# One layer of a gated encoder with three branches on one Trainium2 core: memory keys and values kept unsplit in DRAM, branch input loaded at other products, nine small buffers

## The chip, the cores and the metric

The kernel runs on one core of a Trainium2 chip. The metric is the device time of one launch, in microseconds. It is compared by the median of several runs. The engines carry short names in every table: PE is TensorE (matmuls and transposes; PEld is its loading of weights), DVE is VectorE, ACT is ScalarE, POOL is GpSimd and SP is SyncE, which here only issues DMAs. [...]

## The reference, cut to what matters

One layer is applied to two groups with the same weights: a prompt of 1024 tokens and a sample of 512, each 1024 wide, each with its own 256 memory tokens.

```python
def cross_attention(xq, mem_n, w_mem_kv):
    kv = mem_n @ w_mem_kv                                   # 256 x 1024
    mk = kv[..., :X_WIDTH].reshape(B, M, N_X_HEADS, X_HEAD_DIM)
    mv = kv[..., X_WIDTH:].reshape(B, M, N_X_HEADS, X_HEAD_DIM)
    q = xq.reshape(B, L, N_X_HEADS, X_HEAD_DIM)
    s = jnp.einsum('blhd,bmhd->bhlm', q, mk) * (X_HEAD_DIM ** -0.5)
    p = jax.nn.softmax(s, axis=-1)
    return jnp.einsum('bhlm,bmhd->blhd', p, mv).reshape(B, L, X_WIDTH)

def encoder_layer(x, mem, ...):
    z = rms_norm(x, ln_pre) @ w_in        # cut into inputs and gates of the branches, and merge logits
    ...
    cross_out = cross_attention(xq, rms_norm(mem, ln_mem), w_mem_kv)
    branches = (pool_out * silu(pool_gate), attn_out * silu(attn_gate), cross_out * silu(x_gate))
    gates = sigmoid(merge_logits.reshape(B, L, 3, 1024) + b_merge)
    merged = sum(gates[:, :, n] * (branches[n] @ w_branch[n]) for n in range(3))
    return x + rms_norm(merged @ w_out, ln_post)
```

## The kernel before

All data is float32. Most products are made of three matmuls: both operands are split into a rounded high part and the rest, and `mm3` adds high times high, high times low and low times high (L127). The function `split` makes the two parts: ScalarE writes the high part as a copy (L166), VectorE subtracts it from the original (L163). The parts are kept in tiles of 128 x 2048 (`M`, 14 buffers) for activations, and in `whi` and `wlo` for weights, which `weights` loads into `raw` and splits.

Tiles come from pools that rotate: `U` (128 x 1024, seven buffers), `M`, `HU` (128 x 512, eight buffers, tag hu), `RAW`, and small ones for statistics (`S(n)`, one set of eight for each number of columns). A new tile waits until all readers of the buffer's former content are done. In PSUM `A` has three tiles of 128 x 1024 and `B` two of 128 x 512.

The program is written once in the order of the stages, and a scheduler puts each engine's instructions into a fixed order from it, with priorities (`tc.high_priority`) that pull some of them forward. Each engine works through its own list strictly in order, SP through its list of DMAs too.

The stages, in order of time:

1. `mem_phase` computes keys and values of the memory for both groups, some 10 to 75 us, woven with the steps of `long_h`, which normalises the prompt's input and makes the seven operands of a fast scheme of block products (`put` splits them; L267 and L280 are its differences and sums). Keys: four products of 128 x 512 in PSUM; `evacuate(c)` multiplies each by the norm (L720) into a tile of HU, splits it into two more, and stores high and low parts side by side into DRAM (`mkd`, one tensor for each group, 128 x 2048). Values: four products; ScalarE scales each into its high part (L759), VectorE makes the low part (L760), both are stored (`mvd`).
2. Projections of the prompt and of the sample (`products`, `plain`), 80 to about 700 us. The sums of L336 to L339 and the additions of L441 belong to them.
3. `stream`: a list of units, attention first, then cross attention of the two prompt blocks, attention of the sample, cross attention of the sample. Each unit goes through five steps at fixed distances (load ahead, scores, hand, turn, values), and between the steps matmuls of the remaining projections fill TensorE. In attention the weights of a row block are normalised by POOL and copied by a DMA from one U tile into another (`hand`, L819) before TensorE transposes them. `cross(b, ...)` has four units, one for each head c. `ahead(c)` loads the queries of a head into HU and splits them (L950, L951); at c = 0 it also loads the keys, high and low in one load of 1 MB into an M tile, at c = 2 the values likewise. So they are loaded three times each: for prompt block 0, prompt block 1 and the sample. `scores(c)` multiplies (12 matmuls of 256 columns), ScalarE takes exponentials (L972), POOL normalises (L976), `turn` transposes and splits, `values(c)` multiplies and gates (L998) and the result goes to DRAM as the third branch's output.
4. `branches` and `merge`: for each of three blocks of 512 tokens and each branch in the order 0, 2, 1, eight products (d = 0 to 7) of the branch's output with its weights; L1063 multiplies each by its merge gate, POOL adds (L1065). `chunk(n, c)` loads a quarter (256 KB) of branch n's output into an M tile; the four are split at d = 0 of that branch (`split_pair`). The next branch's chunks are loaded at d = 4 to 7 of the branch before. `gate(i)` loads a merge gate into HU two products ahead. The first block begins as filling of the stream's end.

All loads, and most stores, are issued by SP, in one list (L140 for every load).

## Time and profile before

| | us |
|---|---|
| median of 3 runs | 1477.14 (1474.91 to 1478.22) |
| the profiled execution | 1473.83 |
| its span, first to last instruction | 1472.0 |
| TensorE busy | 1435.9 (98%) |
| VectorE busy | 964.4 (66%) |
| ScalarE busy | 710.6 (48%) |
| GpSimd busy | 277.1 (19%) |

The mean granted clock is 0.993. The core moves 244.94 MB by DMA, at a mean of 166 GB/s. A busy time is the sum of an engine's instructions, so a TensorE that is busy at half its clock counts as busy; the time between the last instruction of the profile and the end of the execution, 1.83 us, lies outside the span. In a timeline row the first number is the start in us from the start of the span, the second the length of the piece, x2 that two instructions of one kind follow each other, and a bracket the idle time ahead with what released it.

### The profile page before, as it was taken

The numbers are of one execution on the slowest core, as the hardware profiler recorded it, in microseconds if no ns is written. First come the engines' busy times: TensorE is split into PE (matmuls) and PEld (weight loads), VectorE is DVE, ScalarE is ACT, GpSimd is POOL, SyncE is SP. The second block draws the span as 40 slices with busy tenths as digits, with TensorE's granted clock in tenths as the row PEclk, the third lists the DMA queues.
The fourth block names the chain that finished last, engine by engine and source line by source line (L and its number), as shares of the span: only waits on it lengthen the run. The fifth ranks groups of instructions, "written<-read, shape, count | busy, mean of one in ns | idle before, by whom it ended". The sixth has DMA issues, their size and how long they took to land. (4 is left out here: it accounts for less than half of the span.)

```text
span 1472.0 us, 19616 instructions
## 1 busy us (share of the span) xinstructions
PE 1435.9 (98%) x7264; PEld 1201.5 (82%) x7264; DVE 964.4 (66%) x1215; ACT 710.6 (48%) x1085; POOL 277.1 (19%) x286
## 2 busy tenths in 40 slices
PE   7989999999999999999999999999999999999998
PEld 5868888888888888788888888888888788888887
DVE  6986586666647674565777676666676564664664
ACT  6454444544434545443666666666666233233232
POOL 1001020110000000210223322233333150240231
PEclk9989999999999999999999999999999999999999
DMA  7523234341422443244655665585356844954852
GB/s 282 158 65 108 86 115 129 108 136 59 130 88 72 152 144 123 85 161 160 244 188 196 215 229 194 189 285 188 128 201 209 295 133 143 316 213 150 318 177 84
DMA packets 97391, 244.94 MB, mean 166 GB/s; under 512 B 10896, under 2 KB 20240, under 8 KB 96528
## 3 DMA queue, kind: packets, MB, share of 16 engines
q1 hardware_dynamic: 88080, 210.14, 42.9%
q10 hardware_dynamic: 9216, 33.56, 5.9%
q8 instruction: 57, 0.93, 0.3%
q14 instruction: 38, 0.31, 0.1%
HBM read 155.57 MB, written 54.53 MB: 143 GB/s over the span
## 5 line engine op out<-in xcount | busy, mean ns | idle before, releaser
L127 PE MATMUL B<-med,whi 128*128 128x512 f32 x1576 | 493.0, 393 | 7.7 <-DVE med L1063 2.8
L127 PE MATMUL A<-med,whi 128*128 128x512 f32 x1200 | 375.8, 394 | 1.9 <-DVE med L163 1.7
L127 PEld LDWEIGHTS B<-med,whi 128*128 128x128 f32 x1576 | 292.0, 188 | 68.2 <-DVE med L1063 3.2
L127 PE MATMUL B<-med,wlo 128*128 128x512 f32 x788 | 308.7, 392 | 0.5 <-DVE wlo L163 0.5
L163 DVE TENSOR_TENSOR wlo<-raw,whi 128x1024 fp32r<-128x1024 f32 (+1 forms) x169 | 205.8, 1218 | 143.5 <-ACT whi L166 140.3
L166 ACT ACTIVATE whi<-raw 128x1024 fp32r<-128x1024 f32 (+1 forms) x169 | 167.2, 990 | 272.1 <-PE A L127 125.5
L127 PEld LDWEIGHTS A<-med,whi 128*128 128x128 f32 x1200 | 224.2, 189 | 48.8 <-DVE med L163 2.2
L127 PE MATMUL A<-med,wlo 128*128 128x512 f32 x600 | 235.5, 392 | 1.8 <-DVE wlo L163 1.8
L127 PEld LDWEIGHTS B<-med,wlo 128*128 128x128 f32 x788 | 148.3, 188 | 32.8 <-DVE wlo L163 1.3
L163 DVE TENSOR_TENSOR med<-A,med 128x1024 fp32r<-128x1024 f32 (+1 forms) x93 | 112.9, 1215 | 34.1 <-ACT med L166 32.6
L127 PEld LDWEIGHTS A<-med,wlo 128*128 128x128 f32 x600 | 113.4, 189 | 26.2 <-DVE wlo L163 2.1
L188 POOL TENSOR_SCALAR s<-s 128x16 f32<-128x16 f32 (+3 forms) x17 | 7.5, 444 | 667.6 <-DVE s L581 332.5
L166 ACT ACTIVATE med<-A 128x1024 fp32r<-128x1024 f32 x92 | 94.2, 1025 | 76.4 <-PE A L131 76.0
L812 POOL TENSOR_SCALAR u<-u,s 128x1024 f32<-128x1024 f32 x64 | 72.2, 1128 | 211.7 <-DVE s L811 173.6
L1065 POOL TENSOR_TENSOR med<-med,hu 128x512 f32<-128x512 f32 x48 | 77.4, 1627 | 131.6 <-DVE hu L1063 127.6
L808 DVE TENSOR_REDUCE s<-A 128x1 f32<-128x1024 f32 x64 | 77.9, 1217 | 36.5 <-PE A L127 14.4
L127 PE MATMUL A<-whi,med 128*128 128x512 f32 (+1 forms) x352 | 98.2, 360 | 0.0
L810 ACT ACTIVATE u<-A,s 128x1024 f32<-128x1024 f32 x64 | 71.4, 1115 | 40.8 <-issue 23.3
L127 PE MATMUL A<-kt,med 128*128 128x512 f32 x320 | 87.9, 396 | 0.0
L166 ACT ACTIVATE whi<-sum 128x1024 fp32r<-128x1024 f32 x50 | 53.1, 1061 | 68.3 <-PE B L127 36.0
L166 ACT ACTIVATE med<-med 128x1024 fp32r<-128x1024 f32 (+1 forms) x44 | 44.2, 1018 | 76.4 <-POOL med L1065 37.1
L163 DVE TENSOR_TENSOR med<-med,med 128x1024 fp32r<-128x1024 f32 (+1 forms) x50 | 56.4, 1141 | 35.1 <-ACT med L166 31.3
(200 smaller groups left out, 1915.4 us busy)
## 6 DMA issues: line engine op xcount, KB each, us to landing
raw<-wt SPq DMA_DIRECT2D x168, 512.0 KB, 3.7
u<-u ACTq DMA_DIRECT2D x64, 512.0 KB, 3.2
merge<-hu SPq DMA_DIRECT2D x72, 256.0 KB, 2.1
hu<-merge SPq DMA_DIRECT2D x72, 256.0 KB, 4.7
med<-br SPq DMA_DIRECT2D x36, 256.0 KB, 4.9
q<-hu SPq DMA_DIRECT2D x24, 256.0 KB, 2.4
br<-hu SPq DMA_DIRECT2D x24, 256.0 KB, 2.7
med<-q SPq DMA_DIRECT2D x12, 512.0 KB, 4.9
```

The lines of the kernel that those rows point to most:

```text
L127: pe.matmul(out, l, r, **k)
L163: v.tensor_tensor(out, x, hi.bitcast(F32), op=ALU.subtract)
L166: act.activation(hi, x, AF.Copy)
L188: pool.tensor_scalar(ss, ss, EPS, 1.0, op0=ALU.add, op1=ALU.mult)
L808: v.reduce_max(mx[:], a[:], axis=AX.X, negate=True)
L810: act.activation(p, a[:], AF.Exp, bias=mx[:], accum_out=sm[:])
L812: pool.tensor_scalar(p, p, rc[:], 1.0, op0=ALU.mult, op1=ALU.mult)
L1065: pool.tensor_tensor(at, at, sg[:], op=ALU.add)
```

## The change

Memory keys and values: `evacuate` and the loop at the end of `mem_phase` store the unsplit product. `mkd` and `mvd` have half the size. `cross` loads them into a U tile at c = 0 (keys) and c = 2 (values) and splits them into an M tile at c = 1 and c = 3. A dictionary that both prompt blocks share keeps the split tiles, so block 1 neither loads nor splits; the sample has its own. Branch input: chunks are loaded at d = 2 to 5 instead of 4 to 7. Buffers: HU has nine instead of eight, and the small tiles of 1, 2 and 4 columns share one set of ten.

```diff
     def S(n):
-        return st.tile([P, n], F32, tag=f"s{n}", bufs=3 if n == 16 else 8, name=nm("s"))
+        w, bufs = (16, 3) if n == 16 else (4, 10)
+        return st.tile([P, w], F32, tag=f"s{w}", bufs=bufs, name=nm("s"))[:, :n]
...
         def evacuate(c):
-            t, hi, lo = HU(), HU(F32R), HU(F32R)
+            t = HU()
             with tc.high_priority(EVAC):
                 v.tensor_tensor(t[:], b[c], sp[:], op=ALU.mult)
-                split(hi[:], lo[:], t[:])
             for g in range(2):
-                for s, x in enumerate((hi, lo)):
-                    o = s * D + c * NMEM
-                    nc.sync.dma_start(mkd[g][:, o:o + NMEM], x[:, g * NMEM:(g + 1) * NMEM].bitcast(F32))
+                nc.sync.dma_start(mkd[g][:, c * NMEM:(c + 1) * NMEM], t[:, g * NMEM:(g + 1) * NMEM])
...
         for t in range(TT):
-            hi, lo = HU(F32R), HU(F32R)
+            x = HU()
             with tc.high_priority(EVAC):
-                act.activation(hi[:], b[t], AF.Copy, scale=r[:, t:t + 1])
-                v.scalar_tensor_tensor(lo[:], b[t], r[:, t:t + 1], hi[:].bitcast(F32), op0=ALU.mult, op1=ALU.subtract)
-            for s, x in enumerate((hi, lo)):
-                o = s * D + t % 2 * BLK
-                nc.sync.dma_start(mvd[t // 2][:, o:o + BLK], x[:].bitcast(F32))
+                act.activation(x[:], b[t], AF.Copy, scale=r[:, t:t + 1])
+            nc.sync.dma_start(mvd[t // 2][:, t % 2 * BLK:(t % 2 + 1) * BLK], x[:])
...
-            if c in (0, 2):
-                k, src = ("mk", mkd) if c == 0 else ("mv", mvd)
-                t = M()
-                load(t[:].bitcast(F32), src[:])
-                state[k] = [t[:, i * D:(i + 1) * D] for i in range(2)]
+            k, src = ("mk", mkd) if c < 2 else ("mv", mvd)
+            if c % 2 == 0 and k not in mem:
+                mem[k] = U()
+                load(mem[k], src[:])
+            elif c % 2 and not isinstance(mem[k], list):
+                t, x = M(), mem[k]
+                mem[k] = [t[:, i * D:(i + 1) * D] for i in range(2)]
+                split(*mem[k], x)
...
-                if d >= 4 and n != order[-1]:
-                    chunk(order[order.index(n) + 1], d - 4)
+                if 2 <= d < 6 and n != order[-1]:
+                    chunk(order[order.index(n) + 1], d - 2)
...
-    units += [u for b in range(2) for u in cross(b, sc, mkd[1], mvd[1])]
-    units += pairs_of(scs, kts, vts) + cross(0, scs, mkd[0], mvd[0])
+    mem = {}
+    units += [u for b in range(2) for u in cross(b, sc, mkd[1], mvd[1], mem)]
+    units += pairs_of(scs, kts, vts) + cross(0, scs, mkd[0], mvd[0], {})
...
-NU, NM, NHU, NRAW, NW = 7, 14, 8, 3, 2
+NU, NM, NHU, NRAW, NW = 7, 14, 9, 3, 2
```

Line numbers move by one or two: L163 becomes L164, L166 becomes L167, L267 becomes L268, L441 becomes L442, L1063 becomes L1061.

The scheduler also puts other instructions into another order. VectorE at about 65 to 80 us, before: `sum` are operands of the projections (L336 to L339), L267 and L280 make `long_h`'s operands, hu_124 is a product's evacuation, and med_82 is the first split that TensorE waits for at 80 us.

```order
60 L760 SCALAR_TENSOR_TENSOR hu_102_578<-A_69_389,s_21_143,hu_101_577 128x512
61 L760 SCALAR_TENSOR_TENSOR hu_104_584<-A_70_390,s_21_143,hu_103_583 128x512
62 L339 TENSOR_TENSOR sum_128_737<-raw_112_661,sum_127_736 128x512
63 L267 TENSOR_TENSOR med_18_136<-med_20_138,med_18_136 128x1024
64 L760 SCALAR_TENSOR_TENSOR hu_106_590<-A_70_390,s_21_143,hu_105_589 128x512
65 L163 TENSOR_TENSOR wlo_130_743<-sum_127_736,whi_129_742 128x1024
66 L280 TENSOR_TENSOR med_17_135<-med_18_136,med_17_135 128x1024 x2
67 L267 TENSOR_TENSOR u_84_509<-med_20_138,med_17_135 128x1024
68 L441 TENSOR_TENSOR hu_124_717<-B_125_719,hu_124_717 128x512
69 L163 TENSOR_TENSOR med_82_503<-med_17_135,med_82_503 128x2x512
```

And now, where med_74 is the same split:

```order
55 L268 TENSOR_TENSOR med_18_136<-med_20_138,med_18_136 128x1024
56 L340 TENSOR_TENSOR sum_116_701<-raw_100_625,sum_115_700 128x512
57 L268 TENSOR_TENSOR med_18_136<-med_20_138,med_18_136 128x1024
58 L281 TENSOR_TENSOR med_17_135<-med_18_136,med_17_135 128x1024
59 L164 TENSOR_TENSOR wlo_110_665<-raw_108_662,whi_109_664 128x1024
60 L281 TENSOR_TENSOR med_17_135<-med_18_136,med_17_135 128x1024
61 L164 TENSOR_TENSOR med_74_479<-med_17_135,med_74_479 128x2x512
62 L268 TENSOR_TENSOR u_76_485<-med_20_138,med_17_135 128x1024
63 L164 TENSOR_TENSOR wlo_118_707<-sum_115_700,whi_117_706 128x1024
```

The low parts of the values (L760) are gone, and the split stands ahead of the difference u_76 (u_84 before), of the weight part of the sum and of the evacuation by L442, which follows further down.

SP at the beginning of the cross attention of the prompt, before: mk_1 and mv_1 are the prompt's keys and values, xq the queries, br1 the attention's output, merge the merge gates, wt the weights.

```order
319 L140 DMA med_1568_8418<-mk_1_87 128x2048
320 L140 DMA hu_1579_8474<-xq_1_1_613 128x512
321 L505 DMA merge_0_2_4_4554<-hu_1577_8469 128x512
322 L140 DMA hu_1591_8516<-xq_1_2_614 128x512
323 L140 DMA hu_1605_8593<-xq_1_3_615 128x512
324 L140 DMA med_1593_8521<-mv_1_89 128x2048
325 L140 DMA raw_1711_9166<-wt 128x1024
326 L936 DMA br1_1_2_606<-hu_1575_8452 128x256
327 L140 DMA med_1619_8668<-mk_1_87 128x2048
```

Now:

```order
307 L141 DMA u_1556_8382<-mk_1_87 128x1024
308 L141 DMA hu_1567_8438<-xq_1_1_577 128x512
309 L506 DMA merge_0_2_4_4518<-hu_1565_8433 128x512
310 L141 DMA hu_1580_8483<-xq_1_2_578 128x512
311 L141 DMA hu_1594_8560<-xq_1_3_579 128x512
312 L141 DMA raw_1699_9132<-wt 128x1024
313 L141 DMA u_1582_8488<-mv_1_89 128x1024
314 L931 DMA br1_1_2_570<-hu_1563_8416 128x256
315 L141 DMA hu_1607_8633<-xq_1_0_576 128x512
```

The loads have half the width, the second load of the keys is gone, and the values' load stands behind a weight load.

SP in the first block of the merge, before: br2 is the store of the cross attention's output, br1 the chunks for the last branch, x_gate a gate of the cross attention.

```order
425 L936 DMA br2_0_1_4519<-hu_1951_10361 128x512
426 L140 DMA raw_1989_10560<-wt 128x1024
427 L140 DMA hu_1970_10464<-x_gate_0_3_4529 128x512
428 L140 DMA hu_1973_10476<-merge_1_2_2_642 128x512
429 L140 DMA med_1988_10558<-br1_1_0_604 128x512
430 L140 DMA med_1988_10558<-br1_1_1_605 128x512
431 L140 DMA hu_1978_10499<-merge_1_2_3_643 128x512
432 L140 DMA med_1988_10558<-br1_1_2_606 128x512
433 L936 DMA br2_0_2_4520<-hu_1961_10413 128x512
434 L140 DMA raw_1996_10602<-wt 128x1024
435 L140 DMA hu_1980_10516<-merge_1_2_4_644 128x512
```

Now:

```order
413 L931 DMA br2_0_1_4483<-hu_1942_10336 128x512
414 L141 DMA raw_1979_10534<-wt 128x1024
415 L141 DMA hu_1963_10448<-merge_1_2_2_606 128x512
416 L141 DMA hu_1968_10471<-merge_1_2_3_607 128x512
417 L141 DMA med_1971_10490<-br1_1_0_568 128x512
418 L141 DMA med_1971_10490<-br1_1_1_569 128x512
419 L141 DMA hu_1970_10488<-merge_1_2_4_608 128x512
420 L141 DMA med_1971_10490<-br1_1_2_570 128x512
421 L931 DMA br2_0_2_4484<-hu_1951_10387 128x512
422 L141 DMA med_1971_10490<-br1_1_3_571 128x512
```

The last two chunks move forward; the merge load that waits for the landing of the store at the top (the store reads the buffer which the load takes) is merge_1_2_2 before and merge_1_2_3 now.

## Rows read from the trace of the kernel before

**Rows 1.** The page's engines: busy us, share of the span, instructions.

```profile
PE 1435.9 (98%) x7264; PEld 1201.5 (82%) x7264; DVE 964.4 (66%) x1215; ACT 710.6 (48%) x1085; POOL 277.1 (19%) x286
```

**Rows 2.** Stretches: us, busy (count) of PE, PEld, DVE, ACT, POOL; clock; DMA; GB/s.

```profile
80.00:100.00 20.00, 15.25 (x45) 11.35 (x46) 18.15 (x19) 9.09 (x11) 0.00 (x0) 0.74 0.13 40
...
960.00:1000.00 40.00, 37.34 (x256) 33.67 (x255) 26.73 (x34) 28.20 (x63) 12.58 (x21) 1.00 0.77 265
...
1040.00:1100.00 60.00, 58.86 (x358) 50.69 (x357) 42.58 (x55) 40.89 (x81) 21.52 (x30) 1.00 0.47 163
```

**Rows 3.** Timeline of PE, 78 to 99 us.

```profile
80.49 0.50 PE L127 MATMUL A<-med,whi 128*128 128x512 f32 x1 [1.74 <-DVE med L163]
...
87.02 0.62 PE L127 MATMUL B<-med,whi 128*128 128x512 f32 x2
...
89.84 0.50 PE L127 MATMUL B<-med,whi 128*128 128x512 f32 x1 [1.75 <-ACT med L166]
...
91.30 0.49 PE L127 MATMUL B<-med,whi 128*128 128x512 f32 x1 [0.74 <-DVE med L163]
93.57 0.79 PE L127 MATMUL A<-med,wlo 128*128 128x512 f32 x1 [1.78 <-DVE wlo L163]
94.17 1.05 PE L127 MATMUL A<-med,whi 128*128 128x512 f32 x2
...
98.43 0.91 PE L127 MATMUL B<-med,whi 128*128 128x512 f32 x2
```

**Rows 4.** Timeline of DVE, 37 to 99 us.

```profile
41.88 0.69 DVE L214 TENSOR_TENSOR u<-ident,s 128x512 f32<-128x512 f32 x1 [1.96 <-POOL s L192]
...
77.46 1.22 DVE L267 TENSOR_TENSOR u<-med,med 128x1024 f32<-128x1024 f32 x1
78.61 0.69 DVE L441 TENSOR_TENSOR hu<-B,hu 128x512 f32<-128x512 f32 x1
79.22 2.35 DVE L163 TENSOR_TENSOR med<-med,med 128x1024 fp32r<-128x1024 f32 x2
...
98.24 0.69 DVE L441 TENSOR_TENSOR u<-A,hu 128x512 f32<-128x512 f32 x1 [1.85 <-PE A L127]
```

**Rows 5.** Groups by line and shape, 26 to 99 us: busy, mean ns, idle before.

```profile
L163 DVE TENSOR_TENSOR med<-med,med 128x1024 fp32r<-128x1024 f32 x10 | 11.9, 1220 | 0.0
...
L760 DVE SCALAR_TENSOR_TENSOR hu<-A,s,hu 128x512 fp32r<-128x512 f32 x4 | 2.9, 745 | 0.0
L163 DVE TENSOR_TENSOR hu<-hu,hu 128x512 fp32r<-128x512 f32 x4 | 2.7, 684 | 0.0
...
L166 ACT ACTIVATE med<-med 128x1024 fp32r<-128x1024 f32 x10 | 10.4, 1056 | 5.5 <-DVE med L259 5.5
```

**Rows 6.** Chain that ended last (start, us), and PE's waits, 960 to 1000 us.

```profile
960.09 8.72 DMA u<-u
...
970.01 8.85 DMA u<-u
...
PE A L131 <- DMA u<-u: 2.7, 2, 1.6
```

**Rows 7.** DMA issues of the whole span: count, KB each, median us to landing.

```profile
med<-mk SPq DMA_DIRECT2D x3, 1024.0 KB, 5.9
```

**Rows 8.** Timeline of SP and of ACT at the sample's cross attention.

```profile
1083.72 0.41 SPq L140 DMA_DIRECT2D med<-mk  x1
...
1105.08 0.63 ACT L950 ACTIVATE u<-hu 128x512 fp32r<-128x512 f32 x1 [3.92 <-DMA hu<-xq]
```

**Rows 9.** Chain at the first merge block; then PE's timeline there.

```profile
1142.90 6.29 DMA br<-hu
...
1150.06 4.99 DMA med<-br
...
1158.09 0.73 PE L127 MATMUL B<-med,whi 128*128 128x512 f32 x2 [2.76 <-DVE med L1063]
...
1158.89 0.62 PE L127 MATMUL B<-med,whi 128*128 128x512 f32 x2
```

More of the change, by code (lines that the diff above doesn't have):

```diff
@@ L938, in stream, with cross @@
             nc.sync.dma_start(out, x)
-    def cross(b, sc, mkd, mvd):
+    def cross(b, sc, mkd, mvd, mem):
         bs = slice(b * BLK, (b + 1) * BLK)
@@ L951, in ahead @@
             v.scalar_tensor_tensor(ql, xf[:], XHD ** -0.5, qh.bitcast(F32), op0=ALU.mult, op1=ALU.subtract)
-            if c in (0, 2):
-                k, src = ("mk", mkd) if c == 0 else ("mv", mvd)
-                t = M()
-                load(t[:].bitcast(F32), src[:])
-                state[k] = [t[:, i * D:(i + 1) * D] for i in range(2)]
+            k, src = ("mk", mkd) if c < 2 else ("mv", mvd)
[6 more added lines that the diff above has]
+                split(*mem[k], x)
             state["q", c] = qh, ql
         def scores(c):
-            mk = state["mk"]
+            mk = mem["mk"]
             qh, ql = state.pop(("q", c))
@@ L989, in values @@
         def values(c):
-            pt, mv = state.pop(c), state["mv"]
+            pt, mv = state.pop(c), mem["mv"]
             o = B()
@@ L1158, in encoder_kernel @@
     act.activation(mhalf[:, :1], mhalf[:, 1:2], AF.Copy)
-    mkd, mvd = [[scratch(f"{n}_{g}", [P, 2 * D]) for g in range(2)] for n in ("mk", "mv")]
+    mkd, mvd = [[scratch(f"{n}_{g}", [P, D]) for g in range(2)] for n in ("mk", "mv")]
     h, hs = [], []
```

## The prediction, made before the changed kernel ran

> **What bounds the kernel now.** I read the page's table of engines first. TensorE is busy 1435.9 us, 98% of the span [rows 1]. The change leaves its matmuls as they are, so only the 36 us that are left, and the stretches in which TensorE runs at its lower clock, can be won or lost. Next I cut the span into stretches to see where these 36 us lie [rows 2]. Part of them lies at the start and the end, which no edit here touches. Three other places are where the change works: 80 to 100, where TensorE is busy 15.25 of 20 us at a mean granted clock of 0.74; 960 to 1000, with 37.34 of 40; and a single wait of 2.76 us at 1158.09 [rows 9].
>
> Third, TensorE's own timeline from 80 to 99 [rows 3]. Four waits stand there, 1.74, 1.75, 0.74 and 1.78 us, 6.0 in all, three released by VectorE's subtraction in split (L163) and one by ScalarE's half of it (L166). The rows also show the clock. [...] The stretch has 45 matmuls [rows 2]; at 0.23 they need 10.4 us, so 9.6 of the 20 us are lost, and with the 1.25 us of the first wait that lie before 80 it is 10.9: 6.0 of waiting and 4.9 of clock.
>
> Fourth, VectorE over the same time [rows 4]. It has no pause between 41.88, where one of 1.96 ends, and 96.4, before one of 1.85. It is the engine that is late, and what it does before 79 us sets when TensorE gets its split pieces at 80.
>
> **What the change does, part by part.** I name the shares A to E.
>
> A, the memory phase. Evacuate and the loop at the end of mem_phase no longer split. VectorE loses four subtractions (L163 on hu, 0.684 each) and four of L760 (0.745 each) [rows 5]. One of the L163 stood before the pause, so 3 x 0.684 + 4 x 0.745 = 5.0 us leave the unbroken stretch; neighbours overlap by about 0.07 (77.46 plus 1.22 against 78.61 [rows 4]), which leaves 4.5 us. ScalarE loses four copies that nobody waited for, and keeps the four L759. SP issues 12 stores instead of 24; nobody reads them before the cross attention. The order moves too: the subtraction that TensorE waits for at 80.49 now stands ahead of a difference (L267) and an addition (L441), 1.15 and 0.61 us [rows 4], so it comes 6.3 us earlier, less up to 1.6 us by which VectorE now pauses longer at 39 to 44, where its own rows run out sooner. That wait is gone. What is late next is VectorE again: behind that first subtraction it still has the other splits of the same group, some 17 us of work (79.22 to 96.4), against 10.4 us of matmuls. So the end of the stretch follows VectorE's end, 4.5 us earlier. On top, TensorE may run the last 11 matmuls (93.57 to 98.43 [rows 3]) at full clock: 11 x 0.21 = 2.3 us. I take 4.5 plus two thirds of that, 6.0. Bounds: 8 if every wait and the low clock go and only a few waits under 0.7 stay; 2.2 from the other side, below, and nothing if the pause at 39 to 44 eats more than I count.
>
> B, one load of memory keys and values for both prompt blocks, of half the size. The chain of waits begins at 960.09 with a copy from SBUF to SBUF that takes 8.72 us and has a second at 970.01 with 8.85 [rows 6], and TensorE's waits for them sum to 2.7 us, 1.62 and 1.04. They were issued just behind a 1 MB load of keys (5.9 us in the median of three [rows 7]) and of values. While the 16 engines were busy they moved 265 GB/s at a share of 0.77 [rows 2], 344 GB/s at full share, so 0.5 MB less ahead of each copy is 1.5 us. The first wait falls to 0.1, the second to none: 2.5 us. Bounds: 2.7, and nothing if other loads fill the room. The two loads of the second prompt block go as well; TensorE waits for nothing there, so they bring nothing.
>
> C, the branch input two products earlier. In the first prompt block it meets the wait of 2.76 us at 1158.09 [rows 9]. That wait is not for want of issue time. A chunk is loaded at 1150.06 because SP's queue stands still until the store of 1142.90 has landed (6.29 us): a merge gate's load ahead of it needs that store's buffer. In the new order the store, a merge load that waits for it, and then the chunks stand in the same sequence; one more small buffer only moves the wait from one merge load to the next. So the first half of the split comes when it came, and the 2.76 us stay. New is that the second half stands directly behind it on ScalarE and VectorE, ahead of a weight split (L166, L163); its last chunk leaves four issues of SP after the second (an estimate of 0.4 us each) and lands about as much later, and TensorE has 24 matmuls, 5.5 us, before it needs that weight: hidden. I take 0. Bounds: 2.8 gained if the store lands sooner, 2.3 lost (1.06 + 1.22) if the last chunk is late. In the five later places of this kind TensorE waits 0.25 us or nothing, and the loads pass only merge and weight loads on SP.
>
> D, the splits that are now made on loading: four, each 1.06 us on ScalarE and 1.22 on VectorE [rows 5], 9.1 us of engine time. In 1040 to 1100 VectorE is busy 42.6 and ScalarE 40.9 of 60 us [rows 2], so there is room; what counts is the place in their queues. In the prompt blocks the keys' split stands before one exponential of the last attention unit, with the load issued some 6 us before by the old times. In the sample's, the keys' load now stands behind all four loads of the first branch input, some 5 us later than 1083.72 [rows 8], and the split must be ready for the sample's first scores; the values' load waits for the keys' split, since it takes its buffer. There ScalarE waited for a query load to 1105.08 anyway [rows 8], and that load now comes before the values', so 3.9 us of idle time take most of the split. I charge 0.5; bounds 0 and 2.3, one split on the path.
>
> E, small buffers: nine instead of eight of HU, and the small tiles of 1, 2 and 4 columns in one set of ten. No large wait of TensorE that I read hangs on them; one HU tile more can only let a load out sooner, and the set of ten serves groups that use three at a time: 0.
>
> **Sum.** -6.0 - 2.5 + 0 + 0.5 + 0 = -8.0 us. The profiled execution took 1473.83 us (span 1472.0), 3.3 us below the median of 1477.14 and 1.1 below the shortest of the three timed runs. It would become 1465.8, and I carry the same 8 us to the median: 1469. With the far bounds (8, 2.7, 2.8, 0, 0) it is 13.5 us, 1463 to 1464, and I give 1463.
>
> **The rivals.**
> First, the clock is not won back. Working the new order through with the old durations leaves TensorE seven waits of 0.3 to 0.7 us between 87 and 95, 3.9 in all, among them one for transposes whose input used to be ready behind other matmuls. Then waits fall by 2.2 us only, and if the 4.9 us at the low level stay, A is 2.2 and the sum -4: 1473. For it: the rows at 89.84 to 93.57 show the low level after waits of 1.75, 0.74 and 1.78 close together [rows 3]. Against it: the wait of 2.76 us at 1158.09 and the two of 960 to 1000 did not lower it: 1.00 over 960 to 1000 [rows 2], two matmuls in 0.62 us at 1158.89 [rows 9]. [...]
>
> Second, the relief is spent elsewhere: ScalarE's halves (1.06 us each [rows 5]) become the late ones from 80 to 95, and the copies at 960 and 970 stay slow since it is not the key loads that hold them up. Then A and B are near nothing: 1477. Against it: ScalarE is busy 9.09 of 20 us there [rows 2].
>
> Third, slower. The new splits stand in queues that run in order. If each load lands as late as the copies of [rows 6], 8.85 us after issue, the key and value loads are not there when ScalarE comes to them, and softmax and the turns of the probabilities queue behind. The price is 2.3 us for each of the four splits and 2.8 us more for the sample's keys, 12 us in all, against 8.5 won: 1480 to 1481. It decides from 11.5 us of new waiting in the two stretches 960 to 1000 and 1085 to 1125. For it: the prompt's keys have only about 2 us to spare and the sample's 1. Against it: the loads are half as big, and both stretches have free time on both engines.
>
> **How the numbers follow.** Forecast 0.55, clock not won back 0.18, relief spent elsewhere 0.13, slower by the splits 0.14. The bound of 0.2% is 3 us, about what a measurement of this kernel can tell from no change. The forecast is faster by more than that, but for 0.03 of it; of the second about two thirds are faster, the rest within; the third is within; the fourth is slower but for a small part. That makes faster 0.66, same 0.21, slower 0.13. The range runs from the far bounds, 1463, over all of the first three cases to 1478; the slower case and a little below are left out.
>
> **What would show it.** A: in VectorE's timeline no L760 and no subtraction on hu, its first pause before 93, TensorE without a wait at 80 and 80 to 100 at a granted clock over 0.85; waits of 0.3 to 0.7 between 87 and 95 would be the new ones. B: copies at 955 to 965 that land in under 7.5 us, the two waits for them under 0.3. C: still one wait of 2 to 3.5 us between 1145 and 1155, released by L1063's counterpart behind a load. D: four new splits with no TensorE wait over 1 us behind them. I am wrong if TensorE's waits near 960 to 1000 or 1085 to 1125 are named after the new splits or the loads of keys and values, or if 80 to 100 still loses 8 us or more.

## The result, and the profile after

The changed kernel took 1460.69 us in the median of four runs (1459.46 to 1464.49), the kernel before 1476.45 beside it: a ratio of 0.9897, 95% interval 0.9875 to 0.9919, 15.8 us less. The profiled execution took 1459.46 us, its span 1457.6. The forecast was 1469 with a range down to 1463: right in its sign, too small in its size.

The changed kernel was measured twice more, on two chips, each time beside the kernel before: 1463.71 against 1475.07 (0.9926, 0.9914 to 0.9938) and 1464.25 against 1473.94 (0.9934, 0.9918 to 0.9949). So 10 to 16 us are won, and the first measurement is the largest of three; the two later medians lie inside the forecast range, at its lower end, and the first lies below it. Some waits for DMAs also come and go from one execution to the next (1.60 us at 1036 for a gate's load in the trace of the first repetition, none there in that of the second), which matters below: a wait counts as gone only where several traces agree.

First the stretches of the changed kernel that answer to [rows 2]. The columns are the same: us, busy time and count of PE, PEld, DVE, ACT and POOL, granted clock (TensorE's, as a share of the full one), DMA share, GB/s.

```profile
60.00:80.00 20.00, 20.00 (x89) 16.52 (x88) 20.00 (x23) 11.34 (x14) 0.00 (x0) 1.00 0.32 105
80.00:100.00 20.00, 17.05 (x73) 12.42 (x72) 19.31 (x22) 11.14 (x15) 0.00 (x0) 1.00 0.20 66
...
960.00:1000.00 40.00, 40.00 (x271) 36.34 (x270) 31.30 (x39) 31.69 (x76) 17.69 (x27) 1.00 0.59 201
...
1100.00:1160.00 60.00, 56.84 (x277) 47.34 (x276) 37.12 (x44) 23.21 (x38) 10.81 (x14) 1.00 0.86 285
```

The last of these stretches in the kernel before:

```profile
1100.00:1160.00 60.00, 54.77 (x295) 46.30 (x294) 37.82 (x47) 29.59 (x60) 12.64 (x20) 1.00 0.71 235
```

From 80 to 100 TensorE does 73 matmuls where it did 45, at full clock. From 960 to 1000 it has no wait left, and the DMA share fell from 0.77 to 0.59. From 1100 to 1160 3.2 us are still lost, with the DMA engines busier than before (a share of 0.86 against 0.71; the changed kernel is 14 us further on in its work there).

Next the start. TensorE's timeline of the changed kernel, which answers to [rows 3]; a bracket is the idle time ahead and what ended it.

```profile
87.30 0.30 PE L132 MATMUL A<-ident,u 128*128 128x128 f32 x1 [0.76 <-DVE u L442]
88.64 0.50 PE L128 MATMUL A<-med,whi 128*128 128x512 f32 x1 [1.04 <-ACT med L167]
...
93.64 0.50 PE L128 MATMUL A<-med,whi 128*128 128x512 f32 x1 [0.40 <-DVE med L164]
...
95.76 0.98 PE L132 MATMUL A<-ident,u 128*128 128x128 f32 x7 [0.69 <-ACT u L440]
```

Four waits of 2.9 us in all stand where 6.0 stood, and none at 80. VectorE's timeline says why.

```profile
71.11 1.22 DVE L281 TENSOR_TENSOR med<-med,med 128x1024 f32<-128x1024 f32 x1
72.24 1.22 DVE L164 TENSOR_TENSOR med<-med,med 128x1024 fp32r<-128x1024 f32 x1
73.38 1.22 DVE L268 TENSOR_TENSOR u<-med,med 128x1024 f32<-128x1024 f32 x1
```

The first split that TensorE needs starts at 72.24, where it started at 79.22 [rows 4]: 7.0 us earlier, and TensorE, which ran out of other work at 78.75 in the kernel before, no longer waits. Much later in the program stands a small wait that all kernels have, near 225 us; below it serves as a mark of how far TensorE has come. First the kernel before, then the changed one:

```profile
229.36 0.54 PE L131 MATMUL B<-identr,u 128*128 128x128 f32 x4 [0.18 <-DVE u L163]
```

```profile
222.29 0.54 PE L132 MATMUL B<-identr,u 128*128 128x128 f32 x4 [0.17 <-DVE u L164]
```

By this mark the start is 7.1 us shorter. A second mark of this kind stands near 617 us, again before and changed:

```profile
617.46 0.73 PE L127 MATMUL B<-med,whi 128*128 128x512 f32 x2 [1.34 <-ACT med L439]
```

```profile
610.25 0.73 PE L128 MATMUL B<-med,whi 128*128 128x512 f32 x2 [1.30 <-ACT med L440]
```

From there to the end of the span (1472.0 and 1457.6) it is 854.5 us before and 847.4 with the change: another 7.2 us, where the forecast had 2.0 behind the start.

Last, from the view of TensorE's waits over the whole span of the changed kernel (us in total, times, longest; the first row is the beginning of the kernel, 7.6 us before any data is there and 2.8 at 25.7).

```profile
PE A L128 <- ACT whi L167: 10.4, 2, 7.6
PE B L128 <- DVE med L1061: 2.3, 1, 2.3
PE B L128 <- ACT med L440: 1.3, 1, 1.3
PE B L128 <- DVE med L164: 1.2, 1, 1.2
...
PE B L128 <- ACT med L167: 0.9, 1, 0.9
...
PE A L132 <- DMA u<-u: 0.2, 1, 0.2
```

The copies (u<-u) cost 0.2 us instead of 3.4 over the whole span (2.7 at 960 to 1000 [rows 6], 0.75 at 882). The wait for the last branch (L1061) is 2.3 us at 1143, where 2.76 stood at 1158 [rows 9]. The kernel before had four more:

```profile
1043.36 0.73 PE L127 MATMUL B<-med,whi 128*128 128x512 f32 x2 [1.14 <-DVE hu L998]
...
1102.15 0.63 PE L131 MATMUL A<-ident,u 128*128 128x128 f32 x4 [0.56 <-DVE med L163]
...
1114.99 1.69 PE L127 MATMUL A<-med,u 128*128 128x256 f32 x12 [0.71 <-ACT u L972]
...
1125.70 1.22 PE L131 MATMUL A<-ident,u 128*128 128x128 f32 x6 [1.08 <-POOL u L976]
```

The three of 0.56, 0.71 and 1.08 us at 1102 to 1126, in the sample's cross attention, are gone in the changed kernel, and so is the one of 1.14 at 1043. One other wait stands in their place:

```profile
1112.08 0.50 PE L128 MATMUL B<-med,whi 128*128 128x512 f32 x1 [0.87 <-ACT med L167]
```

### The profile page after: what moved, and what is told of

Same layout as the page of the kernel before. It is cut to its first block, busy times and chain, and to the rows that moved or that the text cites. A ratio compares the mean times of both kernels' runs of the same rounds, so it can differ in the third digit from the quotient of the medians.

```text
span 1457.6 us, 19545 instructions
## 1 busy us (share of the span) xinstructions
PE 1430.3 (98%) x7264; PEld 1197.1 (82%) x7264; DVE 966.1 (66%) x1211; ACT 711.4 (49%) x1085; POOL 280.3 (19%) x286
## 5 line engine op out<-in xcount | busy, mean ns | idle before, releaser
L167 ACT ACTIVATE whi<-raw 128x1024 fp32r<-128x1024 f32 (+1 forms) x169 | 167.3, 990 | 283.7 <-PE A L128 147.9
L164 DVE TENSOR_TENSOR wlo<-raw,whi 128x1024 fp32r<-128x1024 f32 (+1 forms) x169 | 210.0, 1243 | 138.1 <-ACT whi L167 137.6
L164 DVE TENSOR_TENSOR med<-A,med 128x1024 fp32r<-128x1024 f32 (+1 forms) x93 | 112.8, 1214 | 28.4 <-ACT med L167 26.7
L167 ACT ACTIVATE med<-A 128x1024 fp32r<-128x1024 f32 x92 | 94.2, 1025 | 68.8 <-PE A L132 68.4
L807 POOL TENSOR_SCALAR u<-u,s 128x1024 f32<-128x1024 f32 x64 | 72.1, 1126 | 211.8 <-DVE s L806 174.6
L1063 POOL TENSOR_TENSOR med<-med,hu 128x512 f32<-128x512 f32 x48 | 78.7, 1650 | 130.2 <-DVE hu L1061 130.2
L167 ACT ACTIVATE whi<-sum 128x1024 fp32r<-128x1024 f32 x50 | 52.9, 1061 | 60.3 <-PE B L128 36.5
L164 DVE TENSOR_TENSOR med<-med,med 128x1024 fp32r<-128x1024 f32 (+1 forms) x50 | 55.2, 1115 | 37.8 <-ACT med L167 34.0
L167 ACT ACTIVATE med<-med 128x1024 fp32r<-128x1024 f32 (+1 forms) x44 | 44.3, 1018 | 69.6 <-POOL med L1063 41.7
```

The lines of the kernel that those rows point to most:

```text
L164: v.tensor_tensor(out, x, hi.bitcast(F32), op=ALU.subtract)
L167: act.activation(hi, x, AF.Copy)
L807: pool.tensor_scalar(p, p, rc[:], 1.0, op0=ALU.mult, op1=ALU.mult)
L1063: pool.tensor_tensor(at, at, sg[:], op=ALU.add)
```

## The experiments

All of them started from one question. The start and the copies did about what was forecast; in this first pair of traces some 6 us more were won, and 3.2 of them are the waits at 882, 1043 and 1102 to 1126. Which edit did that: the ninth buffer, the earlier chunks, or fewer and smaller loads?

**One buffer back.** The changed kernel with eight HU buffers.

```diff
-NU, NM, NHU, NRAW, NW = 7, 14, 9, 3, 2
+NU, NM, NHU, NRAW, NW = 7, 14, 8, 3, 2
```

> The changed kernel with eight HU buffers again. Theory 1 (the ninth buffer lets loads of gates and queries out sooner, and that removed the waits of TensorE that stood before at 881, 1043, 1102, 1115 and 1126): three or more of these waits come back, 3 to 5 us, 1464 to 1466. Theory 2 (fewer and smaller loads of keys and values removed them): none comes back, 1460 to 1461.5. The start (80 to 100) and the copies at 960 stay as in the changed kernel under both.

Measured: 1464.12 us (1463.87 to 1466.53), ratio to the kernel before 0.993 (0.9905 to 0.9955). That looked like 3.4 us lost, and the trace had waits for copies of 0.78 at 822 and 0.72 at 876 again. But the waits at 1043 and 1102 to 1126 did not come back, and the two repetitions of the changed kernel gave 0.9926 and 0.9934 with waits for copies of the same kind. So in the changed kernel the ninth buffer is worth nothing that these runs can tell, and theory 1 falls for it.

**The chunks back.** The changed kernel with the branch chunks at products 4 to 7.

```diff
-                if 2 <= d < 6 and n != order[-1]:
-                    chunk(order[order.index(n) + 1], d - 2)
+                if d >= 4 and n != order[-1]:
+                    chunk(order[order.index(n) + 1], d - 4)
```

> The changed kernel with the branch chunks loaded at products 4 to 7 again. My step C (worth nothing, since the chunk waits for the landing of a store): 1460 to 1461.5, one wait of 2 to 3 us before the third branch of the first block, as with the change. Rival (the earlier chunks brought part of the 6 us that I missed, by the order of the loads at the end of the stream): 1462 to 1464, with waits between 1085 and 1145 that the changed kernel has not.

Measured: 1461.97 us (1459.97 to 1465.31), 0.9914 (0.9885 to 0.9943): the same as the changed kernel. The wait for the last branch is 1.39 us, below the 2 to 3 that were expected. Moving the chunks two products ahead brings nothing by itself that these runs can tell, as step C said. The chunks of the last branch stand behind a merge load that waits for a store here too, though this kernel has nine buffers:

```profile
1129.77 0.32 SPq L931 DMA_DIRECT2D br<-hu  x1
...
1131.85 3.34 SPq L141 DMA_DIRECT2D hu<-merge  x2
1135.28 1.53 SPq L141 DMA_DIRECT2D med<-br  x2
```

**Shared, but not smaller.** The kernel before, with the split keys and values loaded once for both prompt blocks.

```diff
...
-                t = M()
-                load(t[:].bitcast(F32), src[:])
-                state[k] = [t[:, i * D:(i + 1) * D] for i in range(2)]
+                if k not in mem:
+                    t = M()
+                    load(t[:].bitcast(F32), src[:])
+                    mem[k] = [t[:, i * D:(i + 1) * D] for i in range(2)]
...
```

> The kernel before, with keys and values still stored split and loaded at 1 MB, but loaded once for both prompt blocks. If the waits for the copies at 960 and 970 (2.7 us) come from the size of the load ahead of them, they stay, and with theory 1 of the first run nothing else changes: 1475 to 1477. If fewer loads are what counts (theory 2), the waits at 1043 and 1102 to 1126 shrink by 2 to 3.5 us: 1473 to 1474. The stretch 80 to 100 stays as before under both.

Measured: 1474.26 us (1468.99 to 1477.7) against 1474.81, ratio 0.9997 (0.998 to 1.0013): no change. Of the waits for copies 0.48 us at 968 and 1.15 at 978 stay; the three waits at 1100 to 1124 stay, 2.5 us. The one at 1043 is not there, but the wait for the last branch is 4.12 us.

**Nine buffers alone.** The kernel before with the ninth buffer and the shared set of small tiles, as in the change.

```diff
-        return st.tile([P, n], F32, tag=f"s{n}", bufs=3 if n == 16 else 8, name=nm("s"))
+        w, bufs = (16, 3) if n == 16 else (4, 10)
+        return st.tile([P, w], F32, tag=f"s{w}", bufs=bufs, name=nm("s"))[:, :n]
...
-NU, NM, NHU, NRAW, NW = 7, 14, 8, 3, 2
+NU, NM, NHU, NRAW, NW = 7, 14, 9, 3, 2
```

> The kernel before with nine HU buffers and the shared set of small tiles, and nothing else of the change. Theory 1: the waits at 881, 1043 and 1102 to 1126 shrink, 3 to 4.5 us, 1472 to 1474. Theory 2: they stay, 1475.5 to 1477. The stretch 80 to 100 keeps its 10.9 us of loss under both.

Measured: 1472.01 us (1469.29 to 1473.69) against 1474.81, 0.9977 (0.9963 to 0.999): 2.8 us less, but not where theory 1 put it. The waits at 829, 883, 980 and 1104 to 1127 are all there. What is gone in this one trace is the wait for the last branch: TensorE has none between 1130 and 1170, though the DMA engines are at a share of 0.92 from 1130 to 1160 (0.86 in the kernel before). SP's timeline of this run shows the place.

```profile
1144.66 0.32 SPq L937 DMA_DIRECT2D br<-hu  x1
1146.73 0.32 SPq L141 DMA_DIRECT2D hu<-merge  x1
1147.14 2.02 SPq L141 DMA_DIRECT2D med<-br  x2
1149.84 0.32 SPq L141 DMA_DIRECT2D hu<-merge  x1
```

The two chunks leave from 1147.14 on, 2.5 us after the store at 1144.66; the merge load that has to wait for its landing leaves behind them, at 1149.84. In the kernel before, that merge load stands ahead of the chunks, and they left from 1149.62 on, 6.7 us after the store of 1142.90 [rows 9].

**The values' load last.** The kernel before, with the values loaded at the fourth head instead of the third.

```diff
-            if c in (0, 2):
+            if c in (0, 3):
```

> The kernel before, with the values' load moved from the third to the fourth head of the cross attention, so that in the sample it is issued behind all four query loads instead of ahead of the last two; nothing else. Theory: the waits at 1102, 1115 and 1126 (2.35 us) come from the last two query loads, which stood behind the values' load of 1 MB and were issued at 1100.15. Then ScalarE's wait of 3.9 us for a query shrinks below 1.5, the three waits together below 0.8, and the time is 1472.5 to 1474 against 1474.8. Rival (the ninth buffer or the split tiles did it): the three waits stay within 0.5 us of their sum, 1474.5 to 1476.

Measured: 1475.49 us (1473.18 to 1477.79) against 1475.07, 1.0006 (0.9996 to 1.0017): no change in time. But the three waits went as the theory had it. SP's timeline of the run, then TensorE's waits in 1095 to 1130 and in 955 to 1165:

```profile
1096.90 0.44 SPq L140 DMA_DIRECT2D hu<-xq  x1
...
1099.41 0.44 SPq L140 DMA_DIRECT2D hu<-xq  x1
1099.95 2.34 SPq L140 DMA_DIRECT2D med<-mv  x1
```

```profile
PE B L127 <- ACT med L166: 0.9, 1, 0.9
...
PE B L127 <- DVE med L1063: 4.0, 1, 4.0
PE A L131 <- DMA u<-u: 2.9, 2, 1.7
```

With the queries (xq) ahead of the values (mv), ScalarE no longer waits for a query (3.92 us in [rows 8]), and of the 2.35 us of waits at 1102 to 1126 none is left; the one of 0.87 us is the one that the changed kernel has at 1112. That the time did not fall by the 1.5 us is not what was expected. In this trace the wait for the last branch is 4.02 us where 2.76 stood, because the chunk there is late by the store that SP waits for: the store left at 1142.52 and took 7.49 us to land (1142.90 and 6.29 in [rows 9]), so an earlier TensorE only waited longer. But that wait was 4.12 us also in the run that only shared the loads, with the three waits in place, so one trace does not show where the 1.5 us went.

**The splits put back.** The changed kernel with all splits of the memory phase computed and thrown away.

```diff
-            t = HU()
+            t, hi, lo = HU(), HU(F32R), HU(F32R)
             with tc.high_priority(EVAC):
                 v.tensor_tensor(t[:], b[c], sp[:], op=ALU.mult)
+                split(hi[:], lo[:], t[:])
...
-            x = HU()
+            x, lo = HU(), HU(F32R)
             with tc.high_priority(EVAC):
                 act.activation(x[:], b[t], AF.Copy, scale=r[:, t:t + 1])
+                v.scalar_tensor_tensor(lo[:], b[t], r[:, t:t + 1], x[:], op0=ALU.mult, op1=ALU.subtract)
```

> The changed kernel with the old splits of keys and values put back in the memory phase, computed but not stored: eight subtractions of VectorE and four copies of ScalarE more. Step A (VectorE's relief before 79 us is what wins the start): the four waits of 6.0 us between 79 and 94 and the low clock come back, 6 to 8 us, 1467 to 1469, with everything after 230 us as in the changed kernel. Rival (the start is won by fewer stores or by nine buffers): 1460 to 1462.

Measured: 1467.24 us (1465.86 to 1467.93), 0.9952 (0.9933 to 0.997). VectorE's timeline of the run:

```profile
77.62 1.22 DVE L268 TENSOR_TENSOR u<-med,med 128x1024 f32<-128x1024 f32 x1
78.76 0.68 DVE L442 TENSOR_TENSOR hu<-B,hu 128x512 f32<-128x512 f32 x1
79.36 2.35 DVE L164 TENSOR_TENSOR med<-med,med 128x1024 fp32r<-128x1024 f32 x2
```

The first split is back at 79.36, behind the same difference and addition as before [rows 4], TensorE waits 2.03 us for it at 80.63, and the granted clock of 80 to 100 is 0.83. The mark near 225 comes at 228.52; before it came at 229.36, with the change at 222.29. Of the four waits of 6.0 us that were expected back, the first came back (2.03 us for 1.74); behind it stand four others of 0.97, 1.04, 0.53 and 0.69 us, 5.3 with the first. Step A holds for work and order together: with the work back, the scheduler also puts the split back behind the difference and the addition, so this run does not part the two. The time is 3.0 to 3.5 us above the two repetitions of the changed kernel, not 6 to 8 (its interval overlaps theirs a little), so the times show less of the start than the mark does.

**Half of them put back.** The changed kernel with the four low parts of the values only (the last line of the diff above and its tile).

```diff
-            x = HU()
+            x, lo = HU(), HU(F32R)
             with tc.high_priority(EVAC):
                 act.activation(x[:], b[t], AF.Copy, scale=r[:, t:t + 1])
+                v.scalar_tensor_tensor(lo[:], b[t], r[:, t:t + 1], x[:], op0=ALU.mult, op1=ALU.subtract)
```

> The changed kernel with only the four low parts of the values put back, computed by VectorE (0.745 us each) but not stored. If VectorE's work ahead of 79 us counts one for one (step A), this costs what is put back: 2.5 to 3.5 us, about half of the 6.5 us of all eight, 1463.2 to 1464.5. If there is room up to a threshold, it costs under 1 us.

Measured: 1468.27 us (1463.61 to 1469.4; 0.9944, 0.9925 to 0.9964), beside 1463.71 for the changed kernel: 4.6 us more, and not less than with all of the work put back (1467.24), so the times do not part the half from the whole. VectorE's timeline of the run:

```profile
77.01 1.22 DVE L164 TENSOR_TENSOR med<-med,med 128x1024 fp32r<-128x1024 f32 x1
78.14 1.22 DVE L268 TENSOR_TENSOR u<-med,med 128x1024 f32<-128x1024 f32 x1
79.28 0.68 DVE L442 TENSOR_TENSOR hu<-B,hu 128x512 f32<-128x512 f32 x1
```

The split keeps its new place ahead of the difference and the addition, and starts 3.7 us later all the same (73.32 in the changed kernel beside it); so the work counts by itself, whatever the order does. The mark near 225 comes at 227.46, where the changed kernel beside it has 223.50: 4.0 us for 3.0 us of work put back. But the granted clock from 80 to 100 is 0.91 here and 1.00 there; against the two traces without work put back that have 0.91 as well (224.82 and 225.30, in the table below) it is 2.2 to 2.6 us. So the relief counts about one for one.

**Chunks issued by ScalarE.**

```diff
-            load(raw[n][:, c * BLK:(c + 1) * BLK], sc[f"br{n}"][c][:, bs])
+            act.dma_start(raw[n][:, c * BLK:(c + 1) * BLK], sc[f"br{n}"][c][:, bs])
```

> The changed kernel with the loads of the branch chunks issued by ScalarE instead of SP. Step C (the chunk stands in SP's list behind a load that waits for the landing of a store): the wait of 2.29 us at 1143 goes or falls below 0.5, 1458 to 1459.5 against 1460.7. Rival (the transfer itself is late since the DMA engines are full, or the M tile is): it stays over 1.5 us. If the issues on ScalarE cost more than they bring, new waits show after 1116.

Measured: 1479.44 us (1475.23 to 1485.91), 1.0036 (1.002 to 1.0053): slower than the kernel before. It did not test step C as I meant it to. ScalarE's timeline of the run, then a row of VectorE's:

```profile
1134.86 1.06 ACT L167 ACTIVATE whi<-raw 128x1024 fp32r<-128x1024 f32 x1 [3.25 <-PE B L128]
1139.79 4.21 ACTq L1012 DMA_DIRECT2D med<-br  x3
1144.39 1.06 ACT L167 ACTIVATE med<-med 128x1024 fp32r<-128x1024 f32 x1 [8.47 <-DMA med<-br]
```

```profile
1139.79 0.69 DVE L1076 TENSOR_SCALAR u<-u 128x1024 f32<-128x1024 f32 x1 [8.81 <-DMA u<-rows]
```

ScalarE issues three of them only at 1139.79, just ahead of the split that needs them, and does nothing else for 8.47 us, from 1135.92 to 1144.39. TensorE waits 6.08 us at 1141, but not for the chunks: it is released by L1061 on VectorE, which stands behind L1076, and that waited 8.81 us for the load of a row of scales for the output (`rows`). SP had issued that load at 1131.99 (at 1150.25 in the changed kernel), and it took 7.8 us to land. Further waits of 0.7 to 1.4 us follow in later blocks. So the run changed more than the place of the chunks, and the slower time can't be put down to ScalarE's late issues alone.

**Not shared, but smaller.** The changed kernel, each prompt block with its own load and split.

```diff
-    units += [u for b in range(2) for u in cross(b, sc, mkd[1], mvd[1], mem)]
+    units += [u for b in range(2) for u in cross(b, sc, mkd[1], mvd[1], {})]
```

> The changed kernel, but each prompt block loads and splits keys and values for itself, at 0.5 MB. If the size of the load ahead of the copies is what removed the waits at 960 and 970 (step B), they stay away, and the second block costs at most 0.5 us: 1460 to 1462. If it takes the sharing too, waits for copies or for a gate (1043 before) come back, 1 to 2.5 us: 1462 to 1463.5.

Measured: 1463.13 us (1461.65 to 1465.87), 0.9929 (0.9904 to 0.9953), the same as the repetitions of the changed kernel. No wait for a copy stands between 960 and 1000. With the run that shared without making smaller, this settles B: the size of the load ahead of the copies counts, the sharing does not. The other parts of the change are out as well: 2.5 us of these waits stay with nine buffers alone and 2.9 with the values' load moved, and none comes back with the chunks or the memory phase's work as before.

**Chunks ahead of the merge load.** The changed kernel with the chunks at products 0 to 3, written ahead of the gate.

```diff
-                gate(i + 2)
-                if 2 <= d < 6 and n != order[-1]:
-                    chunk(order[order.index(n) + 1], d - 2)
+                if 0 <= d < 4 and n != order[-1]:
+                    chunk(order[order.index(n) + 1], d - 0)
+                gate(i + 2)
```

> The changed kernel with the branch chunks loaded at products 0 to 3 and written ahead of the merge gate of the same product. In SP's list the first two chunks of the last branch now stand ahead of the merge load that waits for the landing of a store; in the changed kernel both stand behind it. Theory (that place in the list is what makes the wait of 2.29 us at 1143, and it was what the ninth buffer alone took away in the fourth run): the wait falls below 0.5 us, and the time is 1.5 to 2.3 us below that of the changed kernel beside it. Rival (the transfers are late in any place, since the 16 engines are full there): it stays over 1.5 us, same time.

Measured: 1463.39 us (1461.76 to 1464.6), 0.9919 (0.9906 to 0.9931), beside 0.9926 for the changed kernel: the same. In the trace the chunks leave at 1133.99, 1135.59, 1137.63 and 1140.33 around the stores of 1133.14 and 1139.94, and the wait is 0.94 us at 1145 against 2.59 in the trace of the repetition. It goes through the chunk of 1135.59 now, which took 6.56 us to land. Neither theory came out: the wait is above the 0.5 of the one and below the 1.5 of the other, and the time did not fall. Nor is 0.94 outside what the old place gives (1.01 in the run without sharing), so that the place in SP's list is a cause of the wait is not shown by this run; for it speaks the run with nine buffers alone.

**The changed kernel again**, unchanged, on two chips.

> The changed kernel once more, beside the others of this call: 1459 to 1462 by both theories of the other runs.

> The changed kernel a third time. In the first measurement it took 0.9897 of the time before, in the tenth run 0.9926, and the traces of the two differ by waits for DMAs of 0.4 to 1.6 us at 821, 877, 1036 and 1143. If the true gain is what all traces of changed kernels share against all of the old ones (start 6.5, copies at 960 to 1000 2.5, sample's queries 1.5, last branch about 1: 11.5 us), the ratio is 0.991 to 0.9935 again; if the first measurement was typical, 0.989 to 0.9905.

Measured: 1463.71 us, above the 1459 to 1462 that were expected (1463.24 to 1466.37; 0.9926, 0.9914 to 0.9938) and 1464.25 us (1461.27 to 1466.02; 0.9934, 0.9918 to 0.9949), inside the 0.991 to 0.9935 of what all traces share. The trace of the first has waits that the very first trace had not: 0.94 and 0.58 us for copies at 823 and 877, 1.60 at 1036 for a gate's load. In the second there is 1.19 at 820 and none at 1036. So the waits at 882 and 1043 are not what the change removed: they come and go.

Across all traces, the four kernels with the old memory phase and loads (before, e3, e4, e5) against the changed kernel and its variants:

| | old | changed |
|---|---|---|
| shared wait near 225 us (the start) | 229.4 to 230.2 | 221.6 to 225.3 without work put back (8 traces) |
| waits for copies, 960 to 1000 | 1.6 to 3.0 | none in 10 traces |
| waits in the sample's cross attention | 2.4, 2.5, 2.5; 0.87 with the values last | 0.87 in eight of ten traces, 1.7 and 2.0 in two |
| wait for the last branch | 2.8, 4.1, 4.0; none with nine buffers | 0.9 to 3.2, and 6.1 with ScalarE's issues |
| other waits for copies and gates, 820 to 1045 | 0.5 to 1.9 | 0.2 to 3.1 |

## Why the prediction was right or wrong, point by point

**A, the start: right in its cause and its size, in part by luck in what it is made of.** Forecast 6.0 us; the means of the first row differ by 6.8 (229.9 and 223.2). The first split came 7.0 us earlier where 6.3 less up to 1.6 was said, and putting the work back moved the mark by 5.4 us (228.52 against the mean of 223.2), with about 1 us of it already there at the first matmul, which started at 8.43 in that run instead of 7.3 to 7.6. But the stretch did not follow VectorE's end as I had it. VectorE's first pause did not come before 93; it ended at 96.68:

```profile
96.68 2.36 DVE L164 TENSOR_TENSOR wlo<-sum,whi 128x1024 fp32r<-128x1024 f32 x2 [0.57 <-ACT whi L167]
```

I had 4.5 us from VectorE's earlier end and 1.5 from the clock. In the first trace of the changed kernel the waits fell by 3.1 us, from 6.0 to 2.9, and the other 4 us came with the clock, which is at 1.00 from 80 to 100 where it was 0.74. The seven small waits that I had worked out, 3.9 us in all, were four of 2.9. The rival that the clock is not won back is what happened in part of the executions: two of the eight traces have a granted clock of 0.91 from 80 to 100, and these are the ones that reach the mark at 224.8 and 225.3; the others have 1.00 and come at 221.6 to 223.5. Between the two groups lie 2 to 3 us, where that rival had 4.9 for the low clock. Nearly the same four waits stand in both groups (0.76, 1.04, 0.40 and 0.69 us at a clock of 1.00; 0.75, 1.04, 0.53 and 0.69 at 0.91), so what lowered the clock in two of the eight is not shown. The prediction's 0.23 and 0.21 us a matmul can be held against the trace of the kernel before: from 85.41 to 87.70, at a granted clock of 1.00, matmuls of 512 columns start 0.23 us apart and a row of two takes 0.62; from 94.17 to 98.43, at 0.50, they start 0.43 apart and two take 1.05. No run shows the 0.21: a matmul at the low clock cost 0.20 us more, 2.2 for the 11.

**B, the copies: right.** Forecast 2.5 us of 2.7; none of the waits is left. The copy issued behind the keys' load landed after 6.6 us where it took 8.72 [rows 6]. The reason given, the size of the load ahead, is shown by the pair of runs that shared without shrinking (0.48 and 1.15 us of waits left) and shrank without sharing (none).

**D, the splits on loading and the loads' new order: wrong in sign.** This is the failed step as far as the runs name it. I charged 0.5 us, with 0 as the best case, and named what took 1.5 us of waits away: the last two query loads now come ahead of the values' load. I used it only as cover for the split ("3.9 us of idle time take most of the split") and did not ask what TensorE's three waits of 2.35 us behind that idle time hung on. They hung on it: with the values last and nothing else changed they are gone, and only the 0.87 us at the first chunk stands there. That is 2 us from what I charged, in waits. In time the run that moved only this load gained nothing (1.0006), so what D is worth by itself is not shown. The splits cost little: ScalarE waited 0.2 and 0.4 us for the two loads in the sample. In one trace of ten, the one with half of the work put back, TensorE waited 0.68 us for the split of the sample's keys.

**C, the last branch: right for the chunks, too simple in its reason.** The wait stayed (2.29 for 2.76), because the chunks still stand behind a load that waits for a store, and their earlier place alone is worth nothing that these runs can tell. But I wrote that one more buffer "only moves the wait from one merge load to the next". In the kernel before that is enough: it puts the waiting load behind the first two chunks, and nine buffers alone are worth 2.8 us. In the changed kernel they are worth nothing that can be told, and the chunks stand behind the waiting load with their old products as with the new ones. What in the change puts them there again stays open.

**E** was put at 0 and is 0 in the changed kernel.

**The sum.** The start gave what was forecast; what lies behind it did not. From the mark near 617 to the end of the span the four old traces take 853.3 to 857.4 us and the nine changed ones, without the run with ScalarE's issues, 847.3 to 851.9: 5.5 us less in the mean, where B, C and D summed to 2.0. With D at -1.5 and C at some -0.5 to -1 the same working gives 10.5 to 11 us, near the two repetitions (11.4 and 9.7). Even so the bounds would have reached only to 15.0 us, and the first measurement shows 15.8. The 4 to 6 us by which it is larger than the other two are not assigned to an edit: its trace had fewer of the waits that come and go (0.2 us of copies and none for a gate, against 1.5 and 1.6 in the first repetition), and the kernel before was 1.4 to 2.5 us slower beside it. What made those differ stays open. The range was too narrow by this too: I took three runs of the kernel before for its spread and gave the waits for DMAs one value each.

**The rivals.** The relief was not spent elsewhere, and the splits did not block their queues: the loads of 0.5 MB landed after 5.4 us (keys) and 4.7 (values) in the median of two each, not after the 8.85 that the slower case needed.

## What to carry to other kernels

Where one engine is late, count what stands ahead of the piece that the bound engine waits for: taking that work out paid about one for one here (3.0 us put back cost 2.2 to 2.6 against traces with the same granted clock, 0.91), and the granted clock of the stretch, 0.74 before, was 1.00 in six of eight traces. When a transfer moves ahead of another in an in-order list, follow it to the waits behind it and price them; an idle time of another engine is not only cover, it can be the cause of the next wait (here 2.35 us of TensorE's behind 3.92 of ScalarE's). Then look whether a later wait takes the gain back, and trust the time and not the wait that is gone. A pool with one more buffer does not only shorten a wait, it can move the waiting instruction in the list (here from ahead of two chunks to behind them), so try it again with each edit that moves the same list.

## What the runs showed of the hardware that I had not expected

The same program differs by more between chips and executions than the edits in its last third are worth: 1459.46 to 1466.37 us over 16 runs of the changed kernel, with a mean granted clock between 0.994 and 0.998. Waits for DMAs of up to 1.6 us at fixed places are there in one execution and not in the next. And the transfers at the first merge block are slow: at a DMA share of 0.71 (before) and 0.86 (changed) from 1100 to 1160, the store of 256 KB to DRAM with a load waiting behind it landed after 6.3 us in the kernel before, 4.9 with the change and 7.5 with the values last, 2.7 in the median over the whole span of the kernel before, and SP issued nothing behind such a load until the store had landed. The chain of the changed kernel in that place (start, us):

```profile
1128.71 4.91 DMA br<-hu
...
1133.68 0.32 SPq L141
...
1134.10 1.37 SPq L141
...
1135.52 4.76 DMA med<-br
...
1140.36 1.07 ACT med L167
...
1142.60 0.69 DVE med L1061
```
